# A hybrid pooling / HGRN2 decoder trunk: running products over 32 gates with score blocks of 64, a plain first head, and more work in written order

## The chip, the cores and the metric

The kernel runs on one core of a Trainium2 chip. The metric is the device time of one execution in microseconds. Five engines work side by side: TensorE (PE; its weight loads are shown as PEld), VectorE (DVE), ScalarE (ACT), GpSimd (POOL) and SyncE (SP), which here issues the transfers.

## The reference

The input is 1024 tokens of 1024 float32 values, with 16 learned meta tokens ahead of them (1040 tokens). Layer 0 is a causal pooling mixer, layer 1 is HGRN2, a gated linear recurrence with 16 heads of 128. Each layer is normalized first and added to the residual. In layer 1 the reference computes, for each head:

```python
f = lb32 + (1.0 - lb32) * jax.nn.sigmoid(fp32)
log_f = jnp.log(f)
k = (1.0 - lb32) * jax.nn.sigmoid(-fp32)
# S_t = diag(f_t) S_{t-1} + k_t i_t^T, o_t = S_t^T q_t, in chunks:
bcum = jnp.cumsum(g, axis=2)                       # g is log_f
decay = jnp.exp(jnp.where(causal[:, :, None], rel, -jnp.inf))
scores = jnp.einsum('bhtk,bhsk,bhtsk->bhts', q, k, decay)
```

The lower bound `lb` of the gates comes from `hgrn_lb_logits`. For two layers it is the sigmoid of the difference of its two rows, so the smallest difference tells how small a gate can become, and how many gates can be multiplied before their product leaves the range of float32.

## The kernel before

The tokens lie in two passes of 520 (`TP`), each in two halves of 260 (`CH`). Big products are made from pairs of 512-deep weight blocks by a scheme of seven block products instead of eight (`PRODUCTS`, `product_steps`). Float32 operands are split into a high and a low part (`split`, L169 on ScalarE and L172 on VectorE), and each block product is three matmuls for each of four 128-deep slices, 12 matmuls of 260 columns (L428 to L430). The seven products need sums and differences of the weight blocks (L265, L266, L275, L280) and of the token operands (`make_T`, the T tiles, L309).

`whole` writes the work out in program order. `tick()` follows each product; functions that were put off with `later` and `spread` run at their tick, which is how VectorE, ScalarE and the small matmuls are interleaved with the products. The framework then orders each engine's instructions by priority and readiness; inside `manual_schedule` the order of ScalarE and VectorE is the written one. Each engine and each transfer queue works through its list in order, so a transfer whose data is not ready holds up those behind it on the same queue.

Stages: (1) `tokens(0, ...)` of the first pass in written order: load, square (L358), rstd (L118 on VectorE, L119 on POOL), scaling (L361 or L363), transposes back (L374), `hn` (L379, L382), T tiles. (2) the products of the first weight tile for pass 0, then for pass 1, with the tokens of pass 1 spread over the ticks of pass 0. (3) the other tiles of the input projection, both passes together. (4) the group and output stages of layer 0, for pass 0 and pass 1; in those of pass 1 lie the tokens of pass 0 of layer 1, which add the residual (L351, L355) and store `h` (L357, SP queue). (5) `mixer1`: head 0 pass by pass, since the tokens of pass 1 follow during its pass 0; then heads 1 to 15 with both passes together, the scan of head n-1 spread over the products of head n. (6) `out1`, the output projection with the final norm.

In the scan, `run` multiplies the gates in blocks of 16 with one scan instruction, `inv0` to `inv3` take reciprocals, `scale_q`, `scale_k`, `scale_e` bring q and k into the middle of each pair of blocks, and `score0`, `score1` make all scores within blocks of 32 with eight 128x128 matmuls and a mask (L729, L730). `to32` moves q and k to blocks of 32. `e32` copies the even blocks of k to KE (L689); `l32` and `l64` make the rectangles between blocks of 32 and of 64 (`rect`, L681, copied out at L686) and advance q and k (`advance`, L671 to L673). What follows works on chunks of 128. This form runs if the smallest difference of the logits is at least -3.4, else a slower form.

Tiles of one tag share a fixed number of slots: 36 of `unit`, 5 of split weights `w` (and two more at the start), 3 of raw weights, three double banks for products. `LOOK = 3` weights are split ahead.

## Time and profile before

| what | us |
|---|---|
| median of 3 runs (1734.59 to 1737.88) | 1735.27 |
| the profiled execution | 1739.85 |
| its span, first to last instruction | 1738.1 |
| TensorE busy in it (96%) | 1675.4 |
| VectorE busy (71%) | 1232.9 |
| ScalarE busy (47%) | 816.0 |
| POOL busy (3%) | 56.9 |

A group row of the profile reads: line, engine, operation, output<-input, shapes, count | busy us in all, mean ns of one | idle time of the engine before them and what ended it. Matmuls are pipelined, so their durations overlap; how many start in a stretch tells more than the sum of durations. A float32 128x128 matmul that was not split is shown as two records.

### The profile page before, as it was taken

The page shows a single profiled execution, that of the slowest core. Times are in us where ns is not written, and L with a number is a line of the kernel's source. Part 1 is how long each engine was busy: PE and PEld are TensorE (multiplying, and loading weights), DVE is VectorE, ACT ScalarE, POOL GpSimd, SP SyncE. Part 2 cuts the span into 40 slices and gives each one's busy share as a digit, 9 for nine tenths or more (in the row PEclk, how much of TensorE's full clock was granted, in tenths as well). Part 3 has the DMA queues.
Part 4 walks back from the last instruction along what each step waited for, and adds up shares of the span by engine and source line. Part 5 has one row for each costly group of instructions (what it writes and reads, how often), then busy time and mean ns, then how long its engine had stood idle before and what let it go on. Part 6 is the DMA issues. An engine that isn't in the chain of part 4 may idle for free.

```text
span 1738.1 us, 32004 instructions
## 1 busy us (share of the span) xinstructions
PE 1675.4 (96%) x13059; PEld 1624.1 (93%) x13059; DVE 1232.9 (71%) x1945; ACT 816.0 (47%) x1841; POOL 56.9 (3%) x104
## 2 busy tenths in 40 slices
PE   5899999999999999799999999999999999999997
PEld 4799999999998999699999999999999999988786
DVE  6666677788227724898988888888888888884332
ACT  5633333345226524645645555645555645554221
POOL 1000000000000000000000000000000000000000
PEclk9799999999999999899999999999999999999999
DMA  4133333359337443222212212212212212254321
GB/s 136 50 122 99 99 99 110 99 185 297 94 118 241 117 123 111 67 79 80 68 62 86 86 50 80 68 62 86 86 50 80 68 62 86 88 176 142 111 99 43
DMA packets 191425, 176.53 MB, mean 102 GB/s; under 512 B 7093, under 2 KB 164485, under 8 KB 191269
## 3 DMA queue, kind: packets, MB, share of 16 engines
q1 hardware_dynamic: 191269, 174.40, 31.8%
q8 instruction: 105, 1.72, 0.4%
q14 instruction: 51, 0.42, 0.1%
HBM read 132.55 MB, written 41.81 MB: 100 GB/s over the span
## 4 chain that ended last, share of the span: by engine, by line
PE 55%; DVE 3%; ACT 1%; DMA 0%; issue 0%; POOL 0%; DVEq 0%; POOLq 0%
PE mm L428 12%; PE mm L430 11%; PE mm L429 11%; PE mm L990 3%; PE mm L992 3%; PE mm L991 3%; PE at L681 2%; PE at L729 2%; PE at L869 2%; PE at L868 2%; PE at L847 1%; PE at L889 1%; PE at L802 1%; PE at L828 1%; DVE Tl L172 0%
## 5 line engine op out<-in xcount | busy, mean ns | idle before, releaser
L428 PE MATMUL mm<-Th,w 128*128 128x260 f32 x2688 | 778.5, 290 | 18.5 <-ACT P L434 4.1
L430 PE MATMUL mm<-Th,w 128*128 128x260 f32 x2688 | 767.3, 286 | 5.4 <-DVE w L172 5.4
L429 PE MATMUL mm<-Tl,w 128*128 128x260 f32 x2688 | 767.1, 285 | 2.5 <-DVE Tl L172 2.5
L428 PEld LDWEIGHTS mm<-Th,w 128*128 128x128 f32 x2688 | 512.1, 191 | 22.2 <-ACT w L169 4.6
L430 PEld LDWEIGHTS mm<-Th,w 128*128 128x128 f32 x2688 | 512.0, 191 | 7.7 <-DVE w L172 7.5
L429 PEld LDWEIGHTS mm<-Tl,w 128*128 128x128 f32 x2688 | 512.3, 191 | 3.4 <-DVE Tl L172 3.3
L172 DVE TENSOR_TENSOR w<-raw,w 128x512 fp32r<-128x512 f32 x346 | 232.0, 685 | 177.4 <-ACT w L169 169.9
L169 ACT CAST w<-raw 128x512 fp32r<-128x512 f32 x346 | 210.1, 620 | 165.8 <-PE mm L553 110.5
L551 PE MATMUL mm<-a,w 128*128 128x260 f32 x512 | 145.0, 283 | 0.0
L552 PE MATMUL mm<-a,w 128*128 128x260 f32 x512 | 144.9, 283 | 0.0
L553 PE MATMUL mm<-a,w 128*128 128x260 f32 x512 | 144.3, 282 | 0.0
L434 ACT COPY P<-mm 128x520 f32<-128x520 f32 (+1 forms) x153 | 85.7, 560 | 95.5 <-PE mm L430 95.5
L169 ACT CAST w<-S 128x512 fp32r<-128x512 f32 x100 | 60.2, 621 | 109.9 <-PE mm L430 56.1
L710 DVE RECIPROCAL F<-X 128x260 f32<-128x260 f32 x64 | 111.3, 1759 | 0.0
L990 PE MATMUL mm<-woh,w 128*128 128x512 f32 x256 | 101.3, 396 | 0.7 <-DVE hres L1017 0.7
L991 PE MATMUL mm<-wol,w 128*128 128x512 f32 x256 | 100.8, 394 | 0.0
L992 PE MATMUL mm<-woh,w 128*128 128x512 f32 x256 | 100.6, 393 | 0.0
L552 PEld LDWEIGHTS mm<-a,w 128*128 128x128 f32 x512 | 96.7, 189 | 0.0
L551 PEld LDWEIGHTS mm<-a,w 128*128 128x128 f32 x512 | 96.4, 188 | 0.0
L553 PEld LDWEIGHTS mm<-a,w 128*128 128x128 f32 x512 | 96.3, 188 | 0.0
L551 PE MATMUL mm<-u,w 128*128 128x260 f32 x256 | 74.0, 289 | 4.9 <-DVE hn L382 3.1
L119 POOL TENSOR_TENSOR rstd<-rstd,nhalf 128x1 f32<-128x1 f32 (+4 forms) x44 | 44.2, 1004 | 1023.1 <-DVE rstd L118 1010.2
(156 smaller groups left out, 2514.5 us busy)
## 6 DMA issues: line engine op xcount, KB each, us to landing
raw<-in_hgrn_w_in_dram SPq DMA_DIRECT2D x68, 512.0 KB, 4.2
raw<-in_pool_w_in_dram SPq DMA_DIRECT2D x32, 512.0 KB, 4.6
raw<-in_pool_w_out_dram SPq DMA_DIRECT2D x32, 512.0 KB, 4.1
u_dram<-d SPq DMA_DIRECT2D x16, 520.0 KB, 2.7
ur<-u_dram SPq DMA_DIRECT2D x32, 260.0 KB, 5.2
sgh<-s_dram SPq DMA_DIRECT2D x32, 260.0 KB, 4.6
raw<-in_pool_w_grp_dram SPq DMA_DIRECT2D x16, 512.0 KB, 3.9
gl<-g_dram SPq DMA_DIRECT2D x32, 256.0 KB, 5.5
```

Source lines behind the costliest of these rows:

```text
L169: act.copy(hi, src)
L172: vec.tensor_tensor(lo, src, hi.bitcast(F32), sub)
L428: pe.matmul(o, lhsT=w[:, 0, ks], rhs=th[:, k], start=first, stop=False, **kw)
L429: pe.matmul(o, lhsT=w[:, 0, ks], rhs=tl[:, k], start=False, stop=False, **kw)
L430: pe.matmul(o, lhsT=w[:, 1, ks], rhs=th[:, k], start=False, stop=k == 3, **kw)
L551: pe.matmul(o, lhsT=w[:, 0, ks], rhs=xs[k][:, 0, cs], start=first and k == 0, stop=False)
L552: pe.matmul(o, lhsT=w[:, 0, ks], rhs=xs[k][:, 1, cs], start=False, stop=False)
L553: pe.matmul(o, lhsT=w[:, 1, ks], rhs=xs[k][:, 0, cs], start=False, stop=last and k == 3)
L710: vec.reciprocal(iX[:, s], X[:, s])
L990: pe.matmul(ps[i][nh], lhsT=w[:, 0, ts], rhs=wh[:, s], start=n == 0, stop=False)
L991: pe.matmul(ps[i][nh], lhsT=w[:, 0, ts], rhs=wl[:, s], start=False, stop=False)
L992: pe.matmul(ps[i][nh], lhsT=w[:, 1, ts], rhs=wh[:, s], start=False, stop=n == HEADS - 1)
```

## The change

The gates may now be multiplied in blocks of 32 (`whole(32)`) if the smallest logit difference is at least -2.3, in blocks of 16 from -3.4 on, and by the slow form below that. With 32, the score blocks are 64 wide, `l32` does nothing, and `e32` makes the KE of the 64-level. The meta tokens are a block of their own. Head 0's first pass is computed with eight plain block products (`plain`, `pair4`), which need four weight blocks for each pair and a further token operand, `B12`. In the start stage the squares, rstd and scalings of pass 1's rows are written into the hand-ordered part, and its transposes and T tiles follow at ticks 0 to 7. In layer 1 the token steps come two to a tick. The `h` stores, and head 0's `g` stores of pass 0, are issued by POOL instead of SP. The first factor of the rstd moves from VectorE to POOL for the token rows. The scaling in pass 1 of layer 1 moves from ScalarE to VectorE. Two rows instead of three are loaded ahead, and the memsets of `A` and `Zt` stay at their place in program order.

```diff
-LB_MIN = -3.4
+LB_32, LB_16 = -2.3, -3.4
...
-    def rstd_into(r, ssq, tn, n, dim):
-        vec.tensor_scalar(r[:tn, :n], ssq[:tn, :n], 1.0 / dim, EPS, mul, add)
+    def rstd_into(r, ssq, tn, n, dim, eng=vec):
+        eng.tensor_scalar(r[:tn, :n], ssq[:tn, :n], 1.0 / dim, EPS, mul, add)
         pool.tensor_tensor(r[:tn, :n], r[:tn, :n], nhalf[:tn, :n], ALU.pow)
...
-    vec.tensor_scalar(lm[0:1, 2:3], lm[0:1, 1:2], LB_MIN, None, ALU.is_ge)
+    vec.tensor_scalar(lm[0:1, 2:3], lm[0:1, 1:2], LB_16, None, ALU.is_ge)
+    vec.scalar_tensor_tensor(lm[0:1, 3:4], lm[0:1, 1:2], LB_32, lm[0:1, 2:3], ALU.is_ge, add)
...
+        def pair4(view1, view2):
+            ids = (rawid(view1), rawid(view2))
+            def one(i, j):
+                ensure(ids[i] + j)
+                return split_w(raws[ids[i]][:, j * 512 : j * 512 + 512])
+            feed.extend((lambda: one(0, 0), lambda: one(0, 1), lambda: one(1, 0), lambda: one(1, 1)))
...
-        T_STEPS = (("P1",), ("P2",), ("d12", "P6"), ("P5", "d4"), ("d3", "P7"), ("P3", "P4"))
+        T_STEPS = (("P1",), ("P2",), ("d12", "P6"), ("P5", "d4"), ("d3", "P7"), ("P3", "P4"), ("B12",))
...
-                        nc.sync.dma_start(h_dram[t0 - META : t0 - META + tn], ht[:tn, :D])
+                        pool.dma_start(h_dram[t0 - META : t0 - META + tn], ht[:tn, :D])
                 act.activation(sq[:tn, :D], ht[:tn, :D], AF.Square, accum_out=ssq[:tn, 0:1])
-                rstd_into(r, ssq, tn, 1, D)
-                if ys is None and p == 0:
-                    vec.tensor_scalar(sq[:tn, :D], ht[:tn, :D], r[:tn, 0:1], None, mul)
+                rstd_into(r, ssq, tn, 1, D, pool)
+                def scaled():
+                    if (ys is None) == (p == 0):
+                        vec.tensor_scalar(sq[:tn, :D], ht[:tn, :D], r[:tn, 0:1], None, mul)
+                    else:
+                        act.activation(sq[:tn, :D], ht[:tn, :D], AF.Copy, scale=r[:tn, 0:1])
+                held[i] = sq
+                if lag is None and p == 1:
+                    if pend:
+                        pend.pop()()
+                    pend.append(scaled)
                 else:
-                    act.activation(sq[:tn, :D], ht[:tn, :D], AF.Copy, scale=r[:tn, 0:1])
-                held[i] = sq
+                    scaled()
...
+        def plain(p, m, m2):
+            ws = []
+            for c, names in enumerate((("P1", "P2"), ("B12", "P3"))):
+                b = mmbanks()
+                for i, put in enumerate((m, m2)):
+                    o = b[:, i, :CH]
+                    for j, name in enumerate(names):
+                        if c == 0:
+                            ws.append(need())
+                        w = ws[2 * i + j]
+                        th, tl = T[name][p]
+                        for k in range(4):
+                            ks = slice(k * P, (k + 1) * P)
+                            pe.matmul(o, lhsT=w[:, 0, ks], rhs=th[:, k], start=j == 0 and k == 0, stop=False)
+                            pe.matmul(o, lhsT=w[:, 0, ks], rhs=tl[:, k], start=False, stop=False)
+                            pe.matmul(o, lhsT=w[:, 1, ks], rhs=th[:, k], start=False, stop=j == 1 and k == 3)
+                        if j == 0:
+                            tick()
+                    put(slice(p, p + 1), c, b[:, i : i + 1, :CH], None)
+                    tick()
...
-                    ahead.extend(load_tokens(1, i) for i in range(3))
+                    ahead.extend(load_tokens(1, i) for i in range(2))
...
-                        nc.sync.dma_start(by4(g_dram[n])[:, s, c], o)
+                        (pool if s.start == 0 and s.stop == 1 else nc.sync).dma_start(by4(g_dram[n])[:, s, c], o)
...
                 def e32():
                     tl["KE"] = unit("KE")[:, :SEQ].rearrange("p (h t) -> p h t", h=2)
-                    evens(K0, 32, tl["KE"][:, 0])
+                    if run == 32:
+                        evens(K0, 64, tl["KE"][:, 1])
+                    else:
+                        evens(K0, 32, tl["KE"][:, 0])
                 def l32():
+                    if run == 32:
+                        return
                     rect(Q, tl["KE"][:, 0], 32)
                     advance(Q, K0, 32, Fe[:, 24:56], Fe[:, 0:16])
                     evens(K0, 64, tl["KE"][:, 1])
...
-            spread(steps)
+            spread(steps, 0.5)
             st = {}
             puts = [[consumer(part, 0, st) for part in parts] for parts in ("qg", "fi")]
-            for p in range(2):
-                for put in puts:
-                    products((p,), *put)
-                if p == 0:
-                    flush()
+            for put in puts:
+                plain(0, *put)
+            flush()
+            for put in puts:
+                products((1,), *put)
             A = keep[0][:, :SEQ]
-            pool.memset(A, 0.0)
+            tc.keep_in_program_order(pool.memset(A, 0.0))
...
-            for t in list(range(n)) * 2 + list(range(n, tiles)):
+            for t in range(n):
+                pair4(*view(t))
+            for t in range(tiles):
                 pair(*view(t))
...
             a, b = tk(t0, "P5"), wt()
+            rows(0), rows(1)
             end(a), t0["d4"](), end(b)
             t0["d3"]()
             a, b = tk(t0, "P7"), wt()
+            rows(2)
             end(a), end(b)
             a, b = tk(t0, "P3"), tk(t0, "P4")
+            rows(3)
             end(a)
             a = wt()
+            rows(4)
             end(b), end(a)
             end(wt())
-        spread(tokens(1, nw[0], hts=hts1))
+        spread([lambda i=i: sums(i) for i in range(len(TP[1]))], 0.5)
+        spread([lambda fs=fs: [t1[f]() for f in fs] for fs in T_STEPS[:6]], 1, 2)
...
-        spread(tokens(0, nw[1], hs), 2)
+        spread(tokens(0, nw[1], hs, plain=True), 2)
```

## Rows read from the trace of the kernel before

**Rows 1.** The page: its span, and the first row of busy time by engine.
```profile
span 1738.1 us, 32004 instructions
PE 1675.4 (96%) x13059; PEld 1624.1 (93%) x13059; DVE 1232.9 (71%) x1945; ACT 816.0 (47%) x1841; POOL 56.9 (3%) x104
```
**Rows 2.** Windows: stretch, length, busy us (count) by engine, granted clock, DMA share, GB/s.
```profile
21.00:78.50 57.50, 41.89 (x217) 37.70 (x217) 43.07 (x77) 36.88 (x73) 2.73 (x5) 0.79 0.13 38
676.60:730.60 54.00, 39.45 (x289) 36.47 (x287) 41.02 (x77) 36.49 (x77) 3.30 (x5) 0.91 0.33 104
730.60:752.80 22.20, 20.90 (x156) 20.49 (x157) 17.83 (x34) 12.77 (x29) 0.00 (x0) 0.92 0.40 107
80.00:140.00 60.00, 60.00 (x501) 60.00 (x500) 40.74 (x63) 20.42 (x40) 0.99 (x2) 1.00 0.33 105
933.70:985.90 52.20, 52.20 (x444) 51.98 (x443) 44.01 (x69) 28.61 (x73) 2.05 (x3) 1.00 0.23 72
40.00:50.00 10.00, 6.84 (x33) 6.04 (x32) 4.75 (x12) 9.11 (x17) 1.64 (x3) 0.50 0.41 107
```
**Rows 3.** Timeline of PE in a steady head: start us, us, engine, line, operation.
```profile
939.53 0.28 PE L428 MATMUL mm<-Th,w 128*128 128x260 f32 x1
939.79 1.16 PE L681 MATMUL at<-Q,KE 128*128 128x128 f32 x8
940.70 0.37 PE L429 MATMUL mm<-Tl,w 128*128 128x260 f32 x1
...
943.43 0.28 PE L430 MATMUL mm<-Th,w 128*128 128x260 f32 x1
943.56 1.05 PE L681 MATMUL at<-Q,KE 128*128 128x128 f32 x8
944.37 0.37 PE L428 MATMUL mm<-Th,w 128*128 128x260 f32 x1
```
**Rows 4.** Waits: engine, line <- releaser: us in all, times, longest.
```profile
PEld at L681 <- ACT KE L689: 2.5, 14, 0.2
```
**Rows 5.** Timeline of ACT in the start stage.
```profile
28.39 1.06 ACT L169 CAST Th<-T 128x1040 fp32r<-128x1040 f32 x1 [5.03 <-DVE T L309]
...
39.77 1.05 ACT L358 ACTIVATE sq<-ht 8x1024 f32<-8x1024 f32 x1
40.73 0.19 ACT L358 ACTIVATION_READ_ACCUMULATOR sq<-ht 8x1 f32 x1
...
53.03 1.15 ACT L363 ACTIVATE sq<-ht,rstd 128x1024 f32<-128x1024 f32 x1
```
**Rows 6.** Timeline of DVE in head 0.
```profile
701.56 1.27 DVE L355 TENSOR_TENSOR ht<-ht,at 128x512 f32<-128x512 f32 x2
...
728.98 1.23 DVE L172 TENSOR_TENSOR Tl<-T,Th 128x1040 fp32r<-128x1040 f32 x1
```
**Rows 7.** Windows of tile Tl (PE, PEld, DVE), then of tile T (DVE, ACT).
```profile
676.60:730.60 54.00, 19.45 (x68) 13.18 (x68) 8.70 (x10) 0.91 0.33 104
...
676.60:730.60 54.00, 9.91 (x12) 4.22 (x4) 0.91 0.33 104
```
**Rows 8.** Groups by line, whole span.
```profile
L172 DVE TENSOR_TENSOR w<-raw,w 128x512 fp32r<-128x512 f32 x346 | 232.0, 685 | 177.4 <-ACT w L169 169.9 <-PE at L889 6.6
...
L265 DVE TENSOR_TENSOR S<-raw 128x512 f32<-128x512 f32 x50 | 34.2, 684 | 9.7 <-DMA raw<-in_hgrn_w_in_dram 9.7
...
L361 DVE TENSOR_SCALAR sq<-keep,rstd 128x1024 f32<-128x1024 f32 x2 | 1.5, 753 | 2.3 <-POOL rstd L119 2.3
```
**Rows 9.** Timeline of the SP queue in head 0.
```profile
693.36 0.33 SPq L357 DMA_DIRECT2D h_dram<-ht  x1
693.78 0.38 SPq L98 DMA_DIRECT2D ht<-in_x_dram  x1
```
**Rows 10.** Timeline of POOL: the start stage, then head 0.
```profile
42.38 0.54 POOL L119 TENSOR_TENSOR rstd<-rstd,nhalf 8x1 f32<-8x1 f32 x1 [23.98 <-DVE rstd L118]
...
704.91 0.93 POOL L119 TENSOR_TENSOR rstd<-rstd,nhalf 128x1 f32<-128x1 f32 x1 [9.51 <-DVE rstd L118]
```

More of the change, by code (lines that the diff above doesn't have):

```diff
@@ L327, in make_T, with tokens @@
                 "P6": lambda: put("P6", [d["2"]]), "P5": lambda: put("P5", [d["1"]]), "d4": d4, "d3": d3,
-                "P7": lambda: put("P7", [d["3"]]), "P3": lambda: put("P3", B(1, 1)), "P4": lambda: put("P4", [d["4"]]),
+                "B12": lambda: put("B12", B(0, 1)), "P7": lambda: put("P7", [d["3"]]), "P3": lambda: put("P3", B(1, 1)), "P4": lambda: put("P4", [d["4"]]),
             }
-        T_STEPS = (("P1",), ("P2",), ("d12", "P6"), ("P5", "d4"), ("d3", "P7"), ("P3", "P4"))
-        def tokens(p, w, ys=None, hts=None, lag=2):
-            hn, held = [], {}
+        T_STEPS = (("P1",), ("P2",), ("d12", "P6"), ("P5", "d4"), ("d3", "P7"), ("P3", "P4"), ("B12",))
+        def tokens(p, w, ys=None, hts=None, lag=2, plain=False):
+            hn, held, pend = [], {}, []
             def first(i):
@@ L395, in tokens @@
                 steps.append(step)
-            return steps + [lambda fs=fs: [t[f]() for f in fs] for fs in T_STEPS]
+            return steps + [lambda fs=fs: [t[f]() for f in fs] for fs in T_STEPS[: 7 if plain else 6]]
+        def plain(p, m, m2):
[18 more added lines that the diff above has]
+                    tick()
         def products(*a):
@@ L693, in intra_fast, with last_of, running @@
                 K0 = K[:, META:]
-                F3, Z3 = (a.rearrange("p (b i) -> p b i", i=16) for a in (F, Zt))
+                nb = SEQ // (2 * run)
+                starts = [a[:, META:].rearrange("p (b i) -> p b i", i=run)[:, :, 0] for a in (F, Zt)]
                 X = unit("X")
                 iX = F
-                en = cst.tile([P, 65, 2], F32, tag="en", name="en", bufs=2)
+                en = cst.tile([P, 2 * nb + 1, 2], F32, tag="en", name="en", bufs=2)
                 ends, iends = en[:, :, 0:1], en[:, :, 1:2]
                 ee, eo = ends[:, 1::2], ends[:, 2::2]
-                def run():
-                    vec.tensor_copy(Z3[:, :, 0], F3[:, :, 0])
-                    vec.memset(F3[:, :, 0], 0.0)
-                    vec.tensor_tensor_scan(X, F, Zt, 0.0, mul, add)
-                    act.copy(ends, X.rearrange("p (b i) -> p b i", i=16)[:, :, 15:16])
+                def last_of(ap, o):
+                    e = ap[:, META:].rearrange("p (b i) -> p b i", i=run)[:, :, run - 1 : run]
+                    act.copy(o[:, 1:], e)
+                    act.copy(o[:, 0], ap[:, META - 1 : META])
+                def running():
+                    vec.tensor_copy(starts[1], starts[0])
+                    vec.memset(starts[0], 0.0)
+                    vec.tensor_tensor_scan(X, F, Zt, 1.0, mul, add)
+                    last_of(X, ends)
                 def inv(i):
@@ L1028, in spread @@
             for i, fn in enumerate(steps):
-                later(first + i * gap, fn)
+                later(first + int(i * gap), fn)
         def flush():
@@ L1053, in whole @@
             first, second, t0 = tokens(0, nw[0], hts=hts, lag=None)
+            rows, sums, t1 = tokens(1, nw[0], hts=hts1, lag=None)
             def end(got):
@@ L1092, in whole @@
         products((1,), *c0, kept)
-        if fast:
+        if run:
             later(30, make_mask)
@@ L1108, in whole @@
         mixer1(tokens(1, nw[1], hs, ahead, 3))
-    go = nc.values_load(flag[0:1, 0:1], min_val=0, max_val=1)
-    with tc.If(go > 0) as fork:
-        whole(True)
+    go = nc.values_load(flag[0:1, 0:1], min_val=0, max_val=2)
+    with tc.If(go > 1) as fork:
+        whole(32)
     with fork.Else():
-        whole(False)
+        with tc.If(go > 0) as fork2:
+            whole(16)
+        with fork2.Else():
+            whole(0)
 _INS = [
```

41 lines of the change are left out of this document (22 added, 19 removed).

## The prediction

> **What bounds the kernel now.** I read the page's busy shares first: TensorE is busy for 1675.4 of 1738.1 us [rows 1], so only an edit that takes work from TensorE or shortens its waits can matter. Then I read windows, since a share is a mean over stages. In the stretch 80 to 140 us 501 matmuls take 60 us, 0.120 us each, with no idle time; one HGRN2 head in the steady part is a period of 52.2 us, TensorE busy in all of it, VectorE in 44.0 us, ScalarE in 28.6 us [rows 2]. There the price of an edit is its matmuls and nothing else. Two stretches are different. From 21 to 78.5 us (the first pass and the second pass of the first weight tile) 217 records take 57.5 us; at 0.120 us they would take 26 us. From 676.6 to 752.8 us (head 0, pass by pass, while the tokens of the second half are still normalized) 445 records take 76.2 us where 53 us would do [rows 2]. These two hold nearly all of TensorE's loss: about 31 and 23 us. What TensorE waits for there is VectorE and ScalarE, which normalize, transpose back and split operands.
>
> **Which form will run.** The flag now has three values. With the inputs that the reference draws, the smallest difference of the two rows of lower-bound logits is -2.18, which lies above -2.3, so the form with a running product of 32 runs, and score blocks are 64 wide.
>
> **Part 1, the heads.** With blocks of 64 the step `l32` returns at once. Gone per head: 4 matmuls of the 32-level (8 records), one KE copy and 4 block copies on ScalarE, two 128x512 products and a small one on VectorE. Score matmuls, scan, reciprocals and the scalings keep their size; ScalarE gets two small copies more. In a steady head the records go from a neighbour at 939.53 over the 32-level group at 939.79 to the next at 940.70, and from 943.43 over the 64-level group at 943.56 to 944.37 [rows 3]. Less the usual 0.12, the second group costs 0.82 us and the first 1.05; the first also waits for the KE copy, 2.5 us in 14 heads by the waits [rows 4]. After the change the one group left finds its KE copied two ticks earlier, so that wait has no successor that I can see. Sum: 16 x 0.82 + 2.5 = 15.6 us. Bounds 13.1 (the wait moves to the other group) and 16.8 (1.05 in each head). What VectorE and ScalarE lose here saves nothing by itself: in the steady heads TensorE hides it.
>
> **Part 2, the start.** The rows of the second half (square, rstd, scale) move into the hand-ordered part. Before, ScalarE idles 5.03 us ahead of 28.39 and scales the last row only at 53.03 [rows 5]. Five rows at 1.05 + 0.19 + 1.15 us are 12 us of ScalarE; the new order puts the first two squares and one scale behind the P5 cast (about 32 us), the others between the casts of P7, P3 and P4. Walking ScalarE through in that order, the last scale ends near 49 instead of 54 us and the second-half transposes no longer wait for all of pass 0; the operands of pass 0's last two products come later, near 45 and 48 us, but those products now run at about 49 to 56. The operands of the second half then start some 9 us earlier. Their building is 14 us of VectorE in both stages: 8.70 us of low parts and 9.91 us on the T tiles, of which 4 x 1.23 are in both [rows 6, 7]. I take 8 us. Bounds: 0 (the squares delay the weight casts by as much as the rows gain) and 14.4, VectorE's idle time in the stretch, 57.5 - 43.1 [rows 2]. Small parts inside this range: two memsets leave POOL at the start, the `ssq` scaling goes from VectorE to POOL, and the flag takes one instruction more ahead of the branch (about 0.2 us).
>
> **Part 3, head 0.** Four things change between 676.6 and 752.8 us.
> Added: the first pass takes 8 plain products for each pair where it took 7, 2 x 12 = 24 matmuls, 24 x 0.120 = 2.9 us of TensorE, plus the operand B12 (two casts, two subtractions), built while the pooling output stage holds TensorE full.
> Removed from VectorE: 6 weight splits at 0.685, 8 weight sums at 0.68 [rows 8], 4 evacuation adds (0.4 each, estimated from the two adds of 512 at 701.56 [rows 6]), together 11.2 us; added, five scalings that ScalarE did at 1.15 us [rows 5] and VectorE does at 0.75 [rows 8], 3.8 us. Net -7.5 us of 41.0 in the first pass [rows 2].
> Moved off SP: the stores of `h`. SP issues the load of the last row at 693.78, right behind a store at 693.36 that had to wait for the row before it [rows 9]; that last row is added at 701.56, and the last operand of the second half is done at 728.98 + 1.23 [rows 6]. With the stores on POOL a load waits only for its buffer, and I put the last row's add near 690.
> Compressed: all 14 token steps lie within 7 ticks of 16, so at least 108 matmuls (13 us) are issued behind the last of them.
> TensorE's floor for the first pass is 192 matmuls at 0.120 and 160 transposes at 0.82 / 8 = 0.10 (the 64-level group's price [rows 3]), 39 us against 54. VectorE's remaining 33.5 us no longer fill that. So the first pass may end near 718 instead of 730.6; the second pass has 168 matmuls in 22.2 us and can give 2. That is 13 at best; I take 10, since the scheduler's order leaves gaps. Bounds: -2.9 (only the added matmuls) and 15.
> What may be late next there: two `g` stores and the `h` stores are now queued on POOL ahead of the rstd of the same or a later row, and who waits for the rstd is the scaling and through it the transposes. The page shows no transfer issued by POOL. A POOL rstd takes 0.54 us at 42.38, and 0.93 at 704.91, where VectorE is dense [rows 10]; I put an issue at about 1 us, which the 1.24 us of the square hides [rows 5], with 0.5 as the lower end and 3 as the upper.
> Four of the five weight slots stay held through a plain call, so the next call's weights can be split only as these are freed; one cast and one subtraction (1.3 us) per call may show. It is in the gaps that I left.
>
> **Sum.** 15.6 + 8 + 10 - 0.2 = 33.4 us. The profiled execution takes 1739.85 us (span 1738.1), 4.6 us over the median of 1735.27; the saving is made against its stages and taken from the median: 1735.27 - 33.4 = 1701.9, or 1702 us.
>
> **Rivals.**
> (a) POOL becomes the late link of head 0. For it: the 0.93 us beside dense VectorE work against 0.54 [rows 10]. If each of a row's three POOL operations is held up by one VectorE instruction (up to 1.23 us), a row takes 3 x 1.23 + 2 = 5.7 us on POOL, five rows 28 us, about what the row loads cost now (678 to 706). Then part 3 gives 1 us: 1735.3 - 15.6 - 8 - 1 = 1711. Against it: between rows POOL has nothing else. The Trainium skill, DMA: Bandwidth & Descriptors, section SWDGE vs HWDGE vs iDMA, says that a transfer issued from GpSimd has its descriptors written by software through SBUF, that VectorE can lock it out of that, and that plain transfers belong on SP or ACT; by that rule this case would be the likelier one, and no transfer of this kind is in the trace so far to test it. I give it 20%, with times of 1706 to 1719.
> (b) Both stretches reach their floors: 16.8 + 12 + 15 = 43.8, 1691 us. For it: the idle time of VectorE listed above; against: two engines' orders would both have to fit. 10%.
> (c) The form with 32 gates is not taken, or its new steps bring back what they save: part 1 gives 0, 1735.3 - 18 = 1717 us. The drawn bound lies 0.12 above the limit, so 3%.
> (d) Slower. TensorE starves longer in head 0 and its clock stays at the lower level. The record: 0.50 granted from 40 to 50 us, where TensorE had idled on and off [rows 2], and 0.91 in the first pass of head 0. At 1.2 GHz a matmul costs at most twice 0.120; 360 of them then cost 43 us more, against 23.6 of the other parts: 1735.3 + 19 = 1754 us. It decides from about 225 matmuls at the lower level on (27 us over, 23.6 plus the 3.5 of the bound). For it: four weights held in five slots and two more operand buffers in a pool of 36. Against it: the first pass loses VectorE work. 4%.
> (e) The parts cancel within 0.2%: 3%.
>
> **How the numbers follow.** The forecast has 60%, (a) 20%, (b) 10%, (c) 3%, (d) 4%, (e) 3%. A difference of 0.2% (3.5 us) is about what a measurement of this kernel can tell from no change. Faster: 0.93, same 0.03, slower 0.04. The range reaches from (b), 1691, to the upper end of (a), 1719.
>
> **What would show it.** Part 1: 8 records of the score-rect line per head instead of 16 and a period near 51.2 us; a period of 52 would refute it. Part 2: full rate from about 70 us on instead of 78.5. Part 3: from the first head-0 matmul to the end of its second pass 66 us instead of 76, the last row added near 690 us after allowing for part 2's shift, rstd waits on POOL under 1 us. If POOL's rstd is what ScalarE or VectorE waits for, (a) holds; granted clocks below 0.9 in head 0 speak for (d). The forecast is wrong if the two stretches shrink by less than 8 us together.

## The result, and the profile after

The changed kernel takes 1715.81 us (median of 4 runs, 1714.28 to 1716.46), the kernel before 1736.58 (4 runs, 1734.59 to 1738.82): a ratio of 0.9878, 95% interval 0.9865 to 0.989. The saving is 20.8 us (19.1 to 23.4 by the interval), against a forecast of 33.4. The time lies in the predicted range and the sign is right; the forecast was 14 us too low.

The page of the kernel after, its span and the row of busy time by engine:

```profile
span 1713.5 us, 31678 instructions
PE 1651.1 (96%) x12955; PEld 1603.8 (94%) x12955; DVE 1199.2 (70%) x1865; ACT 784.1 (46%) x1779; POOL 68.6 (4%) x135
```

Beside [rows 1]: TensorE has 104 records and 24.3 us of work less and the span is 24.6 us shorter, so its share of 96% is what it was. By these rows almost all that left the path is busy time of TensorE, hardly any of its idle time. Not all of it is work: in the start 217 records took 41.89 us at a granted clock of 0.79 before [rows 2], and 215 take 36.54 us at 0.94 after.

Windows of the kernel after (stretch, length, busy us and count of PE, PEld, DVE, ACT and POOL, granted clock, DMA share, GB/s): the start, head 0, one steady head, and ten microseconds inside head 0:

```profile
21.00:75.20 54.20, 36.54 (x215) 32.75 (x216) 41.75 (x70) 35.55 (x70) 4.85 (x10) 0.94 0.13 40
674.10:745.60 71.50, 59.42 (x472) 57.50 (x471) 53.77 (x94) 39.84 (x89) 10.01 (x19) 0.93 0.34 111
925.30:976.40 51.10, 51.10 (x435) 51.06 (x435) 42.40 (x66) 27.16 (x68) 2.04 (x3) 1.00 0.24 73
690.00:700.00 10.00, 1.99 (x13) 1.69 (x13) 6.79 (x15) 7.63 (x24) 2.13 (x6) 0.70 0.26 105
```

Against [rows 2], the steady head is full before and after and is 1.1 us shorter, with 9 records fewer. The start and head 0 are shorter, but TensorE still lies idle in them for 17.7 and 12.1 us; it starts only 13 records between 690 and 700 us.

To compare stages between kernels, each is cut at four instructions that all of them have. "Start" is the first ScalarE copy of a 128x520 product bank (77.69 us here). "Group stage" is the time from the eighth to the ninth copy of `h` in layer 0's second pass; the tokens of layer 1's first half are normalized in it. "Head 0" runs from the last copy of `h` in layer 0 to the first 128x520 product copy in layer 1's mixer. "Heads" runs from there to the last score matmul. All in us, from the profiled execution of each kernel:

| kernel | start | group stage | head 0 | heads | span |
|---|---|---|---|---|---|
| before | 81.00 | 75.51 | 76.28 | 802.8 | 1738.1 |
| before, second execution | 79.76 | 74.65 | 76.40 | 802.8 | 1736.0 |
| after | 77.69 | 76.73 | 71.48 | 785.9 | 1713.5 |

The two executions of before differ by up to 1.2 us in a stage; differences of that size are not read below. By this table the heads give 16.9 us, head 0 4.9, the start 2 to 3; the group stage, which no step of the prediction speaks of, gives back 1.2 to 2.1.

### The profile page after: what moved, and what is told of

Its sections match the earlier page's. It is cut to its first block, busy times and chain, and to the rows that moved or that the text cites. A ratio compares the mean times of both kernels' runs of the same rounds, so it can differ in the third digit from the quotient of the medians.

```text
span 1713.5 us, 31678 instructions
## 1 busy us (share of the span) xinstructions
PE 1651.1 (96%) x12955; PEld 1603.8 (94%) x12955; DVE 1199.2 (70%) x1865; ACT 784.1 (46%) x1779; POOL 68.6 (4%) x135
## 4 chain that ended last, share of the span: by engine, by line
PE 71%; DVE 3%; ACT 2%; DMA 1%; issue 1%; POOL 0%; SPq 0%; POOLq 0%; DVEq 0%; ACTq 0%
PE mm L475 12%; PE mm L473 12%; PE mm L474 12%; PE mm L597 5%; PE mm L599 5%; PE mm L598 5%; PE mm L1047 3%; PE mm L1049 3%; PE mm L1048 3%; PE at L781 2%; PE at L926 2%; PE at L925 2%; PE at L904 1%; PE at L946 1%; PE at L727 1%; PE at L854 1%
## 5 line engine op out<-in xcount | busy, mean ns | idle before, releaser
L473 PE MATMUL mm<-Th,w 128*128 128x260 f32 x2632 | 757.0, 288 | 13.5 <-DVE hn L405 6.6
L475 PE MATMUL mm<-Th,w 128*128 128x260 f32 x2632 | 748.4, 284 | 2.0 <-DVE w L174 2.0
L474 PE MATMUL mm<-Tl,w 128*128 128x260 f32 x2632 | 745.7, 283 | 1.8 <-DVE Tl L174 1.8
L473 PEld LDWEIGHTS mm<-Th,w 128*128 128x128 f32 x2632 | 497.7, 189 | 16.2 <-issue 6.5
L474 PEld LDWEIGHTS mm<-Tl,w 128*128 128x128 f32 x2632 | 498.8, 190 | 2.7 <-DVE Tl L174 2.6
L475 PEld LDWEIGHTS mm<-Th,w 128*128 128x128 f32 x2632 | 497.5, 189 | 3.6 <-DVE w L174 3.4
L597 PE MATMUL mm<-u,w 128*128 128x260 f32 x256 | 74.0, 289 | 1.9 <-DVE hn L405 0.9
L598 PE MATMUL mm<-u,w 128*128 128x260 f32 x256 | 73.2, 286 | 0.0
```

Source lines behind the costliest of these rows:

```text
L473: pe.matmul(o, lhsT=w[:, 0, ks], rhs=th[:, k], start=first, stop=False, **kw)
L474: pe.matmul(o, lhsT=w[:, 0, ks], rhs=tl[:, k], start=False, stop=False, **kw)
L475: pe.matmul(o, lhsT=w[:, 1, ks], rhs=th[:, k], start=False, stop=k == 3, **kw)
L597: pe.matmul(o, lhsT=w[:, 0, ks], rhs=xs[k][:, 0, cs], start=first and k == 0, stop=False)
L598: pe.matmul(o, lhsT=w[:, 0, ks], rhs=xs[k][:, 1, cs], start=False, stop=False)
```

## The experiments

Each experiment is timed beside runs of the kernel before on the same chip: 1, 3, 6 and 8 beside a median of 1737.0 us (11 runs), 4, 5, 7 and 9 beside 1738.7 (7 runs), 2, 10, 11 and 12 beside 1736.7 (7 runs). A ratio compares a kernel with the runs beside it. The stages:

| kernel | start | group stage | head 0 | ratio to before (95%) |
|---|---|---|---|---|
| after | 77.69 | 76.73 | 71.48 | 0.9878 (0.9865 to 0.989) |
| 1 blocks of 16 | 77.08 | 77.71 | 71.49 | 0.9971 (0.996 to 0.9982) |
| 2 heads alone | 79.93 | 75.75 | 75.51 | 0.99 (0.9884 to 0.9917) |
| 3 row order of before | 79.55 | 76.47 | 71.05 | 0.9882 (0.9867 to 0.9897) |
| 4 memsets free | 78.68 | 77.28 | 71.4 | 0.9877 (0.9861 to 0.9894) |
| 5 sums in the block | 75.89 | 78.68 | 71.52 | 0.9862 (0.9846 to 0.9879) |
| 6 seven products | 76.70 | 77.32 | 75.12 | 0.9912 (0.9899 to 0.9926) |
| 7 stores on SP | 77.43 | 74.51 | 77.03 | 0.9882 (0.9865 to 0.9898) |
| 8 one step per tick | 77.18 | 77.39 | 72.29 | 0.9885 (0.987 to 0.9901) |
| 9 second before first | 77.51 | 78.89 | 71.80 | 0.9871 (0.9853 to 0.9889) |
| 10 stores split | 76.84 | 73.74 | 71.25 | 0.9861 (0.9844 to 0.9878) |
| 11 both | 76.47 | 74.59 | 71.28 | 0.9865 (0.9848 to 0.9881) |

### 1 and 2. The heads: the change without them, and they without the rest

Experiment 1 keeps every other edit and takes the 16-gate form.

```diff
     with tc.If(go > 1) as fork:
-        whole(32)
+        whole(16)
```

> The changed kernel with the recurrence of 16 gates and score blocks of 32 in the branch that runs; start and head 0 stay as changed. Theory A (the profiles laid side by side: the heads carry 17 of the saving, a period of 52.2 against 51.1 us): the period returns to 52.2 us, the time to about 1733 us, 17 us above the changed kernel, 3 to 5 below the kernel before. Theory B (the forecast's split: heads 15.6, start 8, head 0 10): about 1731 if only the heads were right, and 1718 if the two early stretches had brought their 18 us.

Measured: 1732.57 us (7 runs, 1730.36 to 1734.37). That is 4.4 us under the kernel before, where the changed kernel is 20.8 us under it: by the medians the 32-gate form is worth 16.3 us, by the ratios 16.2. In the profiled executions the heads take 802.5 us here and 785.9 in the kernel after, 16.6 less.

Experiment 2 is the kernel before with the 32-gate form alone.

```diff
-        whole(True)
+        whole(32)
...
-    with fork.Else():
-        whole(False)
+    with fork.Else():
+        with tc.If(go > 0) as fork2:
+            whole(16)
+        with fork2.Else():
+            whole(0)
```

> The kernel before with the 32-gate form alone (flag, scan, blocks of 64); start, head 0, stores, row scaling and memsets as before. Theory A (the parts add): 16 to 17.5 us below the kernel before, ratio 0.990 to 0.9908; head period 51.1 us; start and head 0 as in the kernel before (full rate from 78 to 81 us, head 0 75 to 76 us from the last h copy to its end). Theory B (the heads' gain needs the other edits, since VectorE or ScalarE would else be late in the heads): under 13 us, ratio above 0.9925.

Measured: 1719.94 us (4 runs), 16.8 us under before (17.4 by the ratio); heads 786.1 us, 16.7 less than before. Within the noise the gain of the heads is the same with the other edits and without: the parts add. The other edits together are worth 4 to 5 us (experiment 1 against before: 3.1 to 6.9 by its interval). The busy row of its page:

```profile
PE 1655.7 (96%) x12931; PEld 1606.6 (94%) x12931; DVE 1207.1 (70%) x1898; ACT 792.7 (46%) x1793; POOL 56.0 (3%) x104
```

Against [rows 1], 128 records, 8 for each of 16 heads, and 19.7 us of TensorE are gone, and the span of 1718.2 us is 19.9 us shorter (17.8 against the second execution of before). One steady head of the kernel after, timeline of PE around the group that is left:

```profile
931.71 0.28 PE L475 MATMUL mm<-Th,w 128*128 128x260 f32 x1
931.83 1.05 PE L727 MATMUL at<-Q,KE 128*128 128x128 f32 x8
932.64 0.37 PE L473 MATMUL mm<-Th,w 128*128 128x260 f32 x1
```

From neighbour to neighbour it takes 0.93 us; the second group of [rows 3] took 0.94, and the first, at 1.17 us, is the one that went.

### 3 to 5. The start

Experiment 3 puts the rows of the second half back behind the hand-ordered block.

```diff
-            rows, sums, t1 = tokens(1, nw[0], hts=hts1, lag=None)
...
-            rows(0), rows(1)
...
-        spread([lambda i=i: sums(i) for i in range(len(TP[1]))], 0.5)
-        spread([lambda fs=fs: [t1[f]() for f in fs] for fs in T_STEPS[:6]], 1, 2)
+        spread(tokens(1, nw[0], hts=hts1))
```

> The changed kernel with the rows of the second half taken out of the hand-ordered part again; their steps follow at ticks of the first pass as before. Theory A (of 3.3 us that the start gains in the profiles, 1.7 are there by 27 us and come from POOL without its memsets; the rows' order brings 1.6): 1 to 2 us slower than the changed kernel. Theory B (the order brings most of 8 us): 6 us or more slower.

Measured: 1715.89 us, ratio 0.9882. The time can't be told from that of the kernel after. The start marker stands at 79.55 us; the seven kernels that share the start of the kernel after (it, and experiments 1 and 6 to 10) have theirs at 76.70 to 77.69, so the row order is worth 2 to 3 us there, not 8. The granted clock does not explain it: between 21 and 40 us it is 1.00 in the kernel after and in experiment 7 and 0.50 in the other five, with markers of 77.69 and 77.43 against 76.70 to 77.51. Timeline of ACT in this kernel, the last scaled row and the first operand of the second half:

```profile
53.17 1.15 ACT L377 ACTIVATE sq<-ht,rstd 128x1024 f32<-128x1024 f32 x1 [0.43 <-POOL rstd L120]
...
54.86 0.63 ACT L171 CAST Th<-hn 128x520 fp32r<-128x520 f32 x1
```

The same in the kernel after, with the first evacuations between them, the wait for the later rows' transposes and the marker:

```profile
45.32 1.14 ACT L377 ACTIVATE sq<-ht,rstd 128x1024 f32<-128x1024 f32 x1
46.37 1.21 ACT L402 ACTIVATE hn<-mm,vecs 128x8 f32<-128x8 f32 x6
...
52.60 0.63 ACT L402 ACTIVATE hn<-mm,vecs 128x128 f32<-128x128 f32 x2 [4.21 <-PE mm L397]
53.26 0.63 ACT L171 CAST Th<-hn 128x520 fp32r<-128x520 f32 x1
...
77.69 0.59 ACT L479 COPY P<-mm 128x520 f32<-128x520 f32 x1
```

The last row is scaled 7.9 us earlier, the first operand of that half is cast 1.6 us earlier than in this kernel and 3.2 us earlier than in the kernel before:

```profile
56.49 0.63 ACT L169 CAST Th<-hn 128x520 fp32r<-128x520 f32 x1
```

Between the two stand the transposes and L402, which moves the transposed rows out of their banks. L402 was not written into the block, so ScalarE, which takes its instructions in order, gets to it only behind the whole block at 46.37, although the first transposes ran at 34.31. TensorE's next product waits for that (timeline of PE):

```profile
47.96 0.56 PE L473 MATMUL mm<-Th,w 128*128 128x260 f32 x1 [6.18 <-DVE hn L405]
```

Then it runs the last products of the first pass ahead of the next rows' transposes, and ScalarE waits 4.21 us for these.

Experiment 4 lets the two memsets of head 0 float back to the start of GpSimd's queue.

```diff
-            tc.keep_in_program_order(pool.memset(A, 0.0))
+            pool.memset(A, 0.0)
...
-                tc.keep_in_program_order(pool.memset(Zt, 0.0))
+                pool.memset(Zt, 0.0)
```

> The changed kernel with the memsets of A and Zt free to be placed early again. Theory A (the first 1.5 to 1.7 us of the start's gain came from POOL losing them, since each delayed an rstd by about 1 us): the first matmul of the first product comes about 1 us later, the time 1 to 2 us above the changed kernel. Theory B (the rstd's first factor on POOL is what helped): no change.

Measured: 1717.01 us, ratio 0.9877; start marker 78.68. One to two microseconds by the marker, nothing by the time.

Experiment 5 writes the transposes and evacuations of the first two rows (`sums`) into the block.

```diff
+            sums(0)
             rows(4)
+            sums(1)
...
-        spread([lambda i=i: sums(i) for i in range(len(TP[1]))], 0.5)
+        spread([lambda i=i: sums(i) for i in range(2, len(TP[1]))], 0.5)
```

> The changed kernel with the transposes and hn evacuations of the second half's first two rows written into the hand-ordered part, between the last weight casts. Theory A (in the changed kernel ScalarE evacuates those two rows only at 46.4 us, behind the whole hand-ordered part, though their transposes were done by 40; the product banks stay held and TensorE waits 6.2 us for them): that wait shrinks below 2 us and the start gets 2 to 5 us shorter. Theory B (the weight casts of pass 0's last products set the end of the start): these come 1 to 2 us later and the start gets no shorter.

Measured: 1714.49 us, ratio 0.9862; start marker 75.89, the lowest of all (76.47 with the same edit in experiment 11, and 76.70 at the lowest without it), and the first evacuation at 43.05 instead of 46.37. The two intervals overlap, so a gain in time isn't shown. Nor does the first operand come earlier than the 53.26 us of the kernel after by more than 0.2 us (timeline of ACT; 53.66 in experiment 11):

```profile
53.10 1.15 ACT L171 CAST Th<-hn 128x520 fp32r<-128x520 f32 x2
```

So the late evacuation of these two rows is not by itself what holds the operand back. The transposes and evacuations of the later rows, still spread over the ticks, stand ahead of it too; which of them sets it was not tried.

### 6 and 7. Head 0: the plain products and the stores

Experiment 6 gives the first pass of head 0 its seven products back, with the weights in pairs and without `B12`.

```diff
-                plain(0, *put)
+                products((0,), *put)
...
```

> The changed kernel with head 0's first pass as seven products again (weights in pairs, no B12); token steps two to a tick, stores on POOL. Theory A (plain products save VectorE work that is on the path there, but the gain was eaten by waits for the transposes of the last rows): head 0 about 5 us longer than in the changed kernel, 1720 us. Theory B (as forecast: 7.5 us of VectorE less 2.9 us of TensorE): 4 to 8 us longer. A rival C: TensorE's added 2.9 us cancel it, no difference.

Measured: 1721.89 us (5 runs, 1718.7 to 1722.83): by the medians the plain form is worth 6 us, though it adds 24 matmuls. The profiled execution, the fastest of the five, shows 3.6 us in head 0. Experiment 7 puts the stores of `h` and `g` back on SP.

```diff
-                        pool.dma_start(h_dram[t0 - META : t0 - META + tn], ht[:tn, :D])
+                        nc.sync.dma_start(h_dram[t0 - META : t0 - META + tn], ht[:tn, :D])
...
-                        (pool if s.start == 0 and s.stop == 1 else nc.sync).dma_start(by4(g_dram[n])[:, s, c], o)
+                        nc.sync.dma_start(by4(g_dram[n])[:, s, c], o)
```

> The changed kernel with the h stores and head 0's g stores issued by SP again. Theory B (the forecast: a row's load waits behind the store of the row before it, which cost about 10 us): head 0 gets 5 us or more longer, 1721 us or above. Theory A (in the changed kernel the loads of the last three rows are issued at 673 to 674.6 us, but rows 3 and 4 are added only at 687.9 and 694.6 us, held by the order on VectorE and ScalarE; a store on SP would delay their loads to about 684 and 689 us, landing 5 us later, just in time): 0 to 2 us. Rival (a), POOL as the late link: faster than the changed kernel by up to 5 us.

Measured: 1717.56 us, ratio 0.9882, no difference in time; but the stages move against each other: head 0 takes 77.03 us, 5.5 more, and the group stage 74.51, 2.2 less. Head 0 in this kernel, timeline of the SP queue:

```profile
688.88 0.32 SPq L370 DMA_DIRECT2D h_dram<-ht  x1
689.29 0.38 SPq L99 DMA_DIRECT2D ht<-in_x_dram  x1
```

and of DVE:

```profile
681.08 1.28 DVE L368 TENSOR_TENSOR ht<-ht,at 128x512 f32<-128x512 f32 x2 [1.77 <-DMA ht<-in_x_dram]
...
695.91 1.28 DVE L368 TENSOR_TENSOR ht<-ht,at 128x512 f32<-128x512 f32 x2
```

The load of the last row stands behind a store, as in [rows 9], and so does the one before it (682.81 behind 682.39). The last row is added 24.5 us into head 0, where before needed 24.7. Only one of the last three adds waits for its load, though, for 1.77 us. In the kernel after SP issues three row loads at once:

```profile
673.12 1.48 SPq L99 DMA_DIRECT2D ht<-in_x_dram  x3
```

and its adds (DVE) wait for no load:

```profile
682.10 1.28 DVE L368 TENSOR_TENSOR ht<-ht,at 128x512 f32<-128x512 f32 x2
687.93 1.28 DVE L368 TENSOR_TENSOR ht<-ht,at 128x512 f32<-128x512 f32 x2
694.63 1.27 DVE L368 TENSOR_TENSOR ht<-ht,at 128x512 f32<-128x512 f32 x2
```

The last is 20.5 us into head 0. So the stores on GpSimd take 4 us off the row chain, of which 1.8 are a wait for a load; how the rest comes about is not shown.

About 1.6 more of the 5.5 us are a side effect of the edit. With those stores gone from GpSimd's list, the two memsets of head 0 run in this kernel beside the last row's scaling (timelines of POOL and DVE):

```profile
699.27 0.95 POOL L975 MEMSET keep<- 128x1024 f32 x1
699.36 2.31 DVE L375 TENSOR_SCALAR sq<-ht,rstd 128x1024 f32<-128x1024 f32 x1 [2.17 <-POOL rstd L120]
```

The second memset follows at 700.16 and takes 0.96 us. In the kernel after the memsets come at 713.51 us, and the same scaling takes 0.75.

Set beside experiment 2, which has neither edit, the two belong together: head 0 takes 75.5 us with neither, 77.0 with plain products alone, 75.1 with the stores on GpSimd alone, and 71.5 with both. (The square is not quite clean: experiment 2 lacks the other small edits of head 0 too, and the 77.0 holds the 1.6 us of the memsets.)

Who waits is in the waits of PE from 674 to 726 us (line <- releaser: us in all, times, longest), of the kernel after:

```profile
PE mm L397 <- DVE sq L375: 7.5, 2, 5.8
```

of the kernel with the stores on SP:

```profile
PE mm L397 <- DVE sq L375: 11.7, 4, 8.0
```

and of the kernel with seven products:

```profile
PE mm L473 <- DVE F L680: 6.7, 1, 6.7
PE mm L397 <- DVE sq L375: 6.1, 1, 6.1
```

With seven products TensorE waits for the rows and then once more, for VectorE to bring the product banks out (L680); plain products take the second wait away, and the stores on GpSimd shorten the first. Either alone leaves the other.

### 8 and 9. The rest of head 0's wait: is it the order of the steps?

What is left of it in the kernel after, timeline of PE:

```profile
686.19 0.28 PE L437 MATMUL mm<-Th,w 128*128 128x260 f32 x1
688.16 1.06 PE L397 MATMUL mm<-ident,sq 128*128 128x128 f32 x8 [1.69 <-DVE sq L375]
689.06 1.04 PE L364 MATMUL at<-ident,h 128*128 128x128 f32 x8
692.29 1.09 PE L397 MATMUL mm<-ident,sq 128*128 128x128 f32 x8 [2.19 <-DVE hn L405]
699.20 1.94 PE L397 MATMUL mm<-ident,sq 128*128 128x128 f32 x8 [5.82 <-DVE sq L375]
700.79 0.56 PE L435 MATMUL mm<-Th,w 128*128 128x260 f32 x1
```

After 48 plain matmuls TensorE comes at 686.19 to the transposes of the last three rows (L397), and the other 144 of the 192 stand behind these until 700.79; from there on they run without a wait of their own until 716.51. That no matmul passes an earlier one is also what the Trainium skill states (PSUM — Partial Sum Buffer, section Engine vs sequencer instructions: matmuls start and complete in program order). The rows go add, square, rstd, scaling, transposes, evacuation. The add needs transposes of its own first (L364), but these are not what holds the last row: they end at 690.10, and its add starts at 694.63. Ahead of it VectorE evacuates the earlier rows, as ScalarE does its share of them, and the row before it was added only at 687.93, behind a `g` for which VectorE waited. Timeline of DVE:

```profile
686.92 0.43 DVE L706 TENSOR_TENSOR g<-mm,sig 128x260 f32<-128x260 f32 x1 [3.55 <-ACT sig L705]
...
693.26 1.46 DVE L405 TENSOR_TENSOR hn<-mm,vecs 128x256 f32<-128x256 f32 x3 [0.36 <-ACT hn L402]
```

Two edits try to put products ahead. Experiment 8 spreads the steps over twice the ticks:

```diff
-            spread(steps, 0.5)
+            spread(steps, 1)
```

> The changed kernel with one token step to a tick in head 0 (14 steps over 14 of 16 ticks). Theory A (two steps to a tick put the transposes of the last rows on TensorE's queue ahead of plain products that could run, 5.8 and 2.2 us of waits in the changed kernel): the waits ahead of the transposes shrink and the stretch gets 2 to 5 us shorter. Theory B (early operands are what counts): the operands of the second half come later and the stretch gets 3 to 6 us longer.

Measured: 1716.54 us, ratio 0.9885, head 0 72.29 us. Neither a gain nor a loss that can be told: one long wait takes the place of several short ones, as the timeline of PE shows:

```profile
703.82 1.94 PE L397 MATMUL mm<-ident,sq 128*128 128x128 f32 x8 [7.46 <-DVE sq L375]
```

The last row's transposes start 30.2 us into head 0, 25.1 in the kernel after; but more products stand ahead of them, and 42.1 us of head 0 remain behind them instead of 46.4. The test is not clean: here too the memsets, at 701.27 and 702.16 us, run beside the last scaling, which takes 2.32 us instead of 0.75. Without that the edit might gain; this was not tried.

Experiment 9 writes a row's transposes ahead of the next row's add in each step.

```diff
+                    if ys is not None and p == 1 and i >= lag:
+                        second(i - lag)
                     if i < n:
                         first(i)
-                    if i >= lag:
+                    if not (ys is not None and p == 1) and i >= lag:
                         second(i - lag)
```

> The changed kernel with each token step of the second half in layer 1 written with the transposes back of the older row ahead of the square and scaling of the newer one. Theory A (in head 0 ScalarE holds the hn evacuation of row 0 from 682 to 690 us behind the square of row 3, which waits for VectorE, which waits for a product of TensorE): row 0's hn comes near 683 us, TensorE's waits of 1.7, 2.2 and 5.8 us ahead of the transposes shrink by 3 to 6 us in all. Theory B (the length of the row chain itself sets it): the last row's scaling stays within 1 us of where it is and nothing is gained.

Measured: 1717.07 us, ratio 0.9871, head 0 71.80 us: no difference. The last row is scaled 24.5 us into head 0, in the kernel after 24.2, as theory B has it. Neither edit shortens head 0, and what sets the rest of it stays open: in experiment 9 the row chain keeps its length, in experiment 8 it gets longer while head 0 hardly does.

### 10 and 11. The group stage: stores split by stage

All eight kernels with the `h` stores on GpSimd in both halves spend 76.5 to 78.9 us in the group stage; those with them on SP (before twice, experiments 2 and 7) 74.5 to 75.8. Experiment 10 uses each queue where it was the better one: SP in the group stage, GpSimd in head 0.

```diff
-                        pool.dma_start(h_dram[t0 - META : t0 - META + tn], ht[:tn, :D])
+                        (pool if p == 1 else nc.sync).dma_start(h_dram[t0 - META : t0 - META + tn], ht[:tn, :D])
```

> The h stores of the first half (issued during the group stage of layer 0's second pass) go back to SP; the h stores of head 0 and the two g stores stay on GpSimd. Theory A (a store helps on GpSimd only where row loads would queue behind it on SP, and costs something in the group stage): the group stage takes 74.5 to 75.5 us between its eighth and ninth h copies' marks against 76.7, head 0 stays at 71.5, the kernel takes 1 to 3 us less than the changed one, ratio 0.986 to 0.987. Theory B (the group stage's 2 us in the run with all stores on SP were its clock or chance): group stage 76 to 78.5, no difference, ratio 0.9875 to 0.9885.

Measured: 1711.33 us (4 runs, 1709.65 to 1714.86), ratio 0.9861; group stage 73.74 us, head 0 71.25. Copies of `h` that bound the group stage, timeline of ACT in the kernel after:

```profile
516.78 0.59 ACT L614 COPY h<-mm 128x520 f32<-128x520 f32 x1 [2.27 <-PE mm L599]
593.51 0.59 ACT L614 COPY h<-mm 128x520 f32<-128x520 f32 x1 [2.20 <-PE mm L599]
```

and with the stores split:

```profile
515.01 0.59 ACT L614 COPY h<-mm 128x520 f32<-128x520 f32 x1 [2.27 <-PE mm L599]
588.75 0.59 ACT L614 COPY h<-mm 128x520 f32<-128x520 f32 x1 [2.20 <-PE mm L599]
```

The place is the last of the stage's rows. TensorE's timeline in the kernel after:

```profile
570.73 1.45 PE L397 MATMUL mm<-ident,sq 120*128 120x120 f32 x8 [4.71 <-ACT sq L377]
```

and with the stores split:

```profile
567.50 1.04 PE L397 MATMUL mm<-ident,sq 120*128 120x120 f32 x8 [1.33 <-ACT sq L377]
```

Experiment 11 adds the edit of experiment 5.

```diff
+                        (pool if p == 1 else nc.sync).dma_start(h_dram[t0 - META : t0 - META + tn], ht[:tn, :D])
...
+            sums(0)
             rows(4)
+            sums(1)
...
```

> The edit of the run before, and the sums of rows 0 and 1 of the second half written inside the hand-ordered block. Theory A (both small gains are real and in different stages): start marker near 76 us, group stage near 75, ratio 0.985 to 0.986, 2 to 4 us below the changed kernel. Theory B (neither is): ratio 0.987 to 0.989.

Measured: 1712.35 us, ratio 0.9865. It has the short group stage (74.59) and no more. That the group stage is shorter with its stores on SP is confirmed by these two kernels; that `sums` in the block brings anything is not. Both kernels are faster than the kernel before by 24 to 25 us. Against the kernel after they are 4.5 and 3.5 us faster by the medians, 3.0 and 2.3 by the ratios, and the group stage is 3.0 and 2.1 us shorter; but the intervals of the ratios overlap (0.9844 to 0.9878 and 0.9865 to 0.989).

### 12. The kernel before once more

> The kernel before once more, for a second look at its stages: start marker and head 0 within 2 us of the first look (81.0 and 76.3 us), head period 52.2. If a stage differs by more, that much of the split of the saving over stages is only the spread between two executions.

Measured: 1737.69 us; start 79.76, head 0 76.40, heads 802.8 us. The 2.2 us between the two executions lie in the start (1.2) and the group stage (0.9): so much of the split over stages is spread, and neither head 0 nor the heads have any of it.

## Why the prediction was right and where it was off

The range held and so did the sign: the heads alone are worth 16 to 17 us, and no stage loses more than 2. That the time lies in the range is in part luck: it lies in the upper part, which was put there for rival (a), and that mechanism is not in the trace. The sum was 12.6 us too large. The prediction called itself wrong "if the two stretches shrink by less than 8 us together"; by the markers they shrink by 7.0 to 8.1, at that edge, where 18 were forecast.

**Part 1, 15.6 us: right.** Experiments 1 and 2 give 16.3 and 16.8 us by the medians, the traces 16.6 to 16.9: the upper bound named. The group that went cost its 1.05 us in all 16 heads; its 0.23 us above the other group make 3.7 us, of which the sum had only the 2.5 that the trace lists as waits. The KE wait of [rows 4] found no successor: the weight loads of the group that is left wait 0.1 us in all. "8 records per head" and "a period near 51.2" came out as 8 and 51.1. That VectorE and ScalarE lose work saved nothing beyond that, as forecast.

**Part 2, 8 us: mis-sized; the start gave 2 to 3.** The step that failed is "The operands of the second half then start some 9 us earlier". The rows did come 7.9 us earlier than in experiment 3, near 45 us even where the prediction had put the last scale near 49; but the first operand came 1.6 us earlier than there, and 3.2 us earlier than before. The walk through ScalarE's order ended with the scalings and left out the transposes and evacuations behind them, the first of which were queued on ScalarE behind the whole block. Experiment 5 moved those up, and the operand still came at 53.10 us: which of the later links holds it is open.

The sign "full rate from about 70 us on instead of 78.5" rested on a misreading of before: there TensorE's last wait of the start ends at 73.86 us, in the kernel after at 69.93 (timelines of PE):

```profile
73.86 0.51 PE L428 MATMUL mm<-Th,w 128*128 128x260 f32 x2 [1.12 <-ACT Th L169]
...
69.93 0.39 PE L475 MATMUL mm<-Th,w 128*128 128x260 f32 x1 [1.06 <-DVE w L174]
```

So the sign came true with 3.9 us, not 8; the marker moved from 80 or 81 to 77.7. And of the 31 us that the prediction counted as lost in this stretch, TensorE was idle for 15.6; the rest is matmuls that ran at a granted clock of 0.79.

**Part 3, 10 us: mis-sized; head 0 gave 4.9 and the group stage took 1.2 to 2.1 back.** Its steps, one by one. The plain form paid in spite of its added matmuls: 6 us by the medians, and what it removes in the trace is the wait of 6.7 us for VectorE. "With the stores on POOL a load waits only for its buffer" fits the trace, in which no add of these rows waits for a load; "the last row's add near 690" was not: it came at 694.63, 20.5 us into head 0 against 24.7 before, where about 13 was forecast. With the loads out of the way the adds wait in VectorE's order, behind a `g` and the evacuations of earlier rows. And "at least 108 matmuls are issued behind the last" of the token steps was taken as a gain of packing; 144 are, and TensorE stands idle ahead of them, 9.7 us in three waits. TensorE's floor of 39 us for the first pass counts its work and not this order: that is the failed step of the estimate. The last plain matmul starts 48.1 us into head 0, where the first pass had about 41 by the forecast and 54 before, and the second pass gave none of its 2 us. (The forecast's own terms, 730.6 less 718 and these 2, make 14.6 us, not "13 at best".) The weight casts that were put at "1.3 us per call" are there: the casts at 703.78 and 705.53 us wait 0.86 and 1.14 us for matmuls of the plain call, but beside the 144; TensorE's only waits from 700.8 us to the end of head 0 are 1.0 and 0.3 us.

The group stage was overlooked. The edit of the stores applies to both halves, and the prediction priced it in head 0 alone. In the group stage of the kernel before two adds wait for their loads, 0.6 and 0.7 us, so there was little to gain; what it costs there is shown (2 to 4 us, experiments 7, 10 and 11), why is not: two of the rows' adds wait 1.6 and 1.9 us for their loads in the kernel after, and one 0.7 us with the stores split. The stores themselves land no later from GpSimd (a median of 4.7 us after issue, against 4.9 from SP in experiment 10); what delays the loads was not tried.

**Rival (a), GpSimd as late link of head 0: not seen.** Its time of 1711 is near the result, its mechanism isn't in the trace. Timeline of POOL in the kernel after:

```profile
683.67 0.60 POOL L370 DMA_DIRECT2D h_dram<-ht  x1 [2.28 <-DVE ht L368]
684.66 0.18 POOL L119 TENSOR_SCALAR rstd<-ssq 128x1 f32<-128x1 f32 x1 [0.38 <-ACT sq L371]
684.92 0.56 POOL L120 TENSOR_TENSOR rstd<-rstd,nhalf 128x1 f32<-128x1 f32 x1
```

A row costs 1.3 us on this engine, not 5.7, and the engine idles 2.28 us before it. The advice of the Trainium skill (DMA: Bandwidth & Descriptors, section SWDGE vs HWDGE vs iDMA), quoted with that rival, that plain transfers belong on SP or ACT, agrees with the group stage and not with head 0. The same section of the Trainium skill also states that VectorE, in its 2-port mode, locks GpSimd out of the memory that holds the descriptors. No run here shows the mode, and the effect is small: beside dense VectorE work an issue takes 0.53 to 0.63 us in head 0, once 0.73 (kernel after and experiment 10); the longest, 0.91 and 0.94 us in experiment 6, lie beside a row scaling on VectorE. **Rival (b)**, both floors at once, needed what failed in parts 2 and 3. **(c)** is refuted by experiment 1, **(d)** by head 0 being shorter although its clock falls: 0.70 is granted between 690 and 700 us, where TensorE waits for the rows, and 0.50 from there to 704.2, the lower of its two levels (1.2 of 2.4 GHz); the matmuls after 700.79 start 0.217 us apart until then and 0.12 later on, some 1.6 us lost.

## What to carry to other kernels

When work is moved earlier on an engine by hand, follow its product to the next instruction of the chain on every engine: here the rows came 8 us earlier and the operands made from them 1.6. A floor from counts is none for a stretch where an in-order engine has waiting transposes ahead of ready products; there the waits have to be priced too, and edits that shorten different links (the loads, the wait for banks) paid here only together. An edit that takes work off one engine moves what is left on it: look at what that now runs beside, as with the memsets of experiments 7 and 8. An edit to a helper that two stages share has to be priced in both: a store on GpSimd took 4 us off the row chain in head 0, and cost 2 to 4 us in the stage where the adds had waited little for their loads.

## What was not expected of the hardware

A 512 KB store issued from GpSimd occupies it for about 0.60 us and SP for 0.32; beside a row scaling on VectorE it took 0.91 (experiment 6). The other way round the effect is larger: a row scaling on VectorE that starts beside a memset on GpSimd took 2.31 and 2.32 us beside two memsets (experiments 7 and 8) and 1.42 beside one (experiment 4, at 13.08 us), where it takes 0.75 otherwise, and ended each time about 0.55 us after the memsets did. In head 0 such a store lands a median 3.0 us after issue (four of them), in the group stage 4.7 (three), while the same tiles' loads take 7.6 and 5.2. Issued from SP it lands 2.9 us after issue in head 0 (experiment 7).
